# The last store of a rotary embedding, as 120 partitions and two transfers of small pieces

## The chip, the core and the metric

The kernel runs on one core of a Trainium2 chip. The metric is the device time of the program in microseconds, the median of several runs. A profile of one execution lies beside them; its span is the time from the first to the last instruction of the core.

## What is computed

The input `x` is (16, 512, 1024) in fp32: 16 batches, 512 positions, 16 heads of 64. Each head is rotated by its position's angle:

```python
x1, x2 = x[..., :half_dim], x[..., half_dim:]
rotated = concatenate([x1 * cos - x2 * sin, x1 * sin + x2 * cos], axis=-1)
```

with `cos` and `sin` of (512, 32), the same for all batches and heads. 33.55 MB are read and as many written, and little is computed on each.

## The kernel before

The 128 partitions of SBUF each hold some consecutive positions. A *row* `u` is one position of each partition, 128 x 1024 elements, 4 KB a partition; there are 64 rows. They are grouped into ten *tiles*: batches 0, 1, 14 and 15 are tiles of their own (4 rows, 16 KB a partition, 2 MB), and the twelve batches between go in pairs (8 rows, 32 KB a partition, 4 MB). The last tile, number 9, is batch 15, rows 60 to 63.

All tiles live in one ring `x_sb` of 40 rows and are changed in place. ACT issues the loads (`load`, L154): as many as the ring holds at the start, and the others when the store of the rows that they overwrite has ended (L195). Then, for each row:

- VectorE multiplies the row by the cosine into PSUM (`t1_ps`, L302).
- GpSimd multiplies the row, halves swapped, by the signed sine into `t2_sb` (L263), mostly two rows in one instruction; for one row of each pair tile VectorE does it (L295).
- The two are added: for 43 rows VectorE adds them back into `x_sb` (`comb`, L313); for 21 rows TensorE adds `t2` to PSUM through an identity matrix (L225), and ACT copies the sum back (L192).

SP only stores. `on_sync` walks the rows; at the last row of a tile it waits until all rows so far are added (`wait_added`, L138 and its neighbours) and issues one transfer for the tile (L162), ten in all. `in_dram` and `in_sbuf` give the two sides; for the last tile each is 128 rows of 16 KB. The store signals a semaphore, +16 when all of it has landed: one of three that ACT waits for, or `sem_rest` for the last six stores. The last instruction of SP waits for all of `sem_rest` (L163); with that the program ends.

SP's stores and ACT's loads go through queues of their own (q1 and q10 in the profile), which are served by the same 16 DMA engines.

## Time and profile before

| | |
|---|---|
| median of 3 runs | 161.18 us (161.16 to 162.24) |
| the profiled execution | 161.04 us |
| its span | 159.6 us |
| busy: VectorE, GpSimd, TensorE, ACT | 81%, 82%, 40%, 15% of the span |
| DMA: 67.25 MB in 3169 packets | 421 GB/s over the span |
| stores (q1), loads (q10) | 48.9%, 49.8% of the 16 engines' span |
| last store issued | 151.9 us |

The share of a queue is the time that its packets took, over 16 engines and the span; the two together leave 1.3% of the engines' time free. In the tables by window below, the columns are the stretch and its length, the busy time of PE, PEld, DVE, ACT and POOL with the number of instructions, the clock granted to TensorE, the busy share of the DMA engines, and GB/s. A packet is one contiguous run of bytes that a DMA engine moves, or a closing packet of 4 bytes that signals a semaphore.

### The profile page before, as it was taken

How to read it: one execution, taken by the hardware profiler on the slowest of the kernel's cores; microseconds unless marked ns; L12 is line 12 of the kernel's file. 1: busy time of each engine (PE TensorE's matmuls, PEld its weight loads, DVE VectorE, ACT ScalarE, POOL GpSimd, SP SyncE). 2: the span in 40 equal slices, each digit the busy share in tenths (PEclk: the TensorE clock that was granted, in tenths of full speed). 3: DMA queues.
4: the chain of work that ended last, by engine and by line, in shares of the span. 5: the costliest groups of instructions: out<-in, count | busy, mean ns of one | idle time of the engine just before them, and what ended most of it. 6: DMA issues, size and time to landing. Idle time of an engine off the chain costs nothing.

```text
span 159.6 us, 499 instructions
## 1 busy us (share of the span) xinstructions
PE 64.4 (40%) x94; PEld 22.2 (14%) x94; DVE 129.6 (81%) x117; ACT 24.3 (15%) x27; POOL 131.7 (82%) x41
## 2 busy tenths in 40 slices
PE   6050017076408870789067400575058506900000
PEld 1020011021102220222021100211021102300000
DVE  0069947999999989998999629999999999556900
ACT  0420002004300250023102040023202310220000
POOL 1069999999999999999999798992999999089400
PEclk9999999759985589557759985589957995585555
DMA  5999999999999999999999999999999999999997
GB/s 144 396 466 472 394 411 431 448 476 402 394 448 406 495 419 402 476 435 402 443 435 435 394 476 435 402 460 394 427 456 448 443 394 423 472 419 435 386 456 300
DMA packets 3169, 67.25 MB, mean 421 GB/s; under 512 B 352, under 2 KB 608, under 8 KB 608
## 3 DMA queue, kind: packets, MB, share of 16 engines
q10 hardware_dynamic: 1728, 33.69, 49.8%
q1 hardware_dynamic: 1440, 33.56, 48.9%
q14 instruction: 1, 0.01, 0.0%
HBM read 33.69 MB, written 33.55 MB: 421 GB/s over the span
## 4 chain that ended last, share of the span: by engine, by line
DMA 61%; DVE 17%; POOL 5%; PE 5%; issue 4%; ACTq 1%; ACT 1%; DVEq 0%; POOLq 0%; SPq 0%
DMA x_sb<-in_x_dram 43%; DMA out_dram<-x_sb 18%; DVE t_ps L302 8%; DVE x_sb L313 7%; POOL t_sb L263 5%; PE t_ps L225 5%; DVE t_sb L295 2%; ACT x_sb L192 1%; ACTq L154 1%; ACTq L175 1%; DVE tab_ps L280 0%; DVEq L312 0%; DVE tab_ps L281 0%; DVEq L299 0%; POOLq L259 0%
## 5 line engine op out<-in xcount | busy, mean ns | idle before, releaser
L263 POOL TENSOR_TENSOR t_sb<-x_sb,s_sb 128x2048 f32<-128x2048 f32 (+1 forms) x35 | 131.0, 3784 | 17.1 <-DMA x_sb<-in_x_dram 8.3
L225 PE MATMUL t_ps<-t_sb,ident 128*128 128x512 f32 x84 | 59.6, 857 | 69.1 <-DVE t_ps L302 56.7
L302 DVE TENSOR_TENSOR t_ps<-x_sb,pair_ps 128x1024 f32<-128x1024 f32 x48 | 57.5, 1221 | 5.2 <-ACT x_sb L192 5.2
L313 DVE TENSOR_TENSOR x_sb<-t_ps,t_sb 128x1024 f32<-128x1024 f32 x43 | 52.2, 1216 | 5.9 <-POOL t_sb L263 5.9
L192 ACT ACTIVATE x_sb<-t_ps 128x1024 f32<-128x1024 f32 x21 | 21.4, 1024 | 107.6 <-PE t_ps L225 99.9
L225 PEld LDWEIGHTS t_ps<-t_sb,ident 128*128 128x128 f32 x84 | 20.3, 267 | 108.2 <-DVE t_ps L302 78.7
L302 DVE TENSOR_TENSOR t_ps<-x_sb,tab_ps 128x1024 f32<-128x1024 f32 x16 | 19.2, 1222 | 2.6 <-DMA x_sb<-in_x_dram 2.5
L295 DVE TENSOR_TENSOR t_sb<-x_sb,tab_ps 128x1024 f32<-128x1024 f32 x6 | 7.3, 1209 | 0.0
L273 DVE COPY tab_ps<-stage 128x128 f32<-128x128 f32 x1 | 0.3, 296 | 7.6 <-DMA stage<-in_cos_dram 7.6
L209 PE MATMUL pair_ps<-stage,pick 128*128 128x256 f32 x4 | 2.0, 667 | 5.1 <-DMA stage<-in_sin_dram 5.1
L202 PE MATMUL t_ps<-zero 128*128 128x512 bf16 x6 | 2.7, 629 | 1.3 <-DVE zero L271 1.3
L178 ACT ACT_TABLE_LOAD x1 | 1.3, 1283 | 5.5 <-issue 5.5
L209 PEld LDWEIGHTS pair_ps<-stage,pick 128*128 128x128 f32 x4 | 1.2, 324 | 6.1 <-issue 6.0
L202 PEld LDWEIGHTS t_ps<-zero 128*128 128x128 bf16 x6 | 0.7, 136 | 2.4 <-DVE zero L271 1.2
L271 DVE MEMSET zero<- 128x256 uint32 x1 | 0.3, 272 | 0.9 <-PEq L346 0.9
L187 ACT ACTIVATE s_sb<-pair_ps 128x256 f32<-128x256 f32 x1 | 0.4, 384 | 1.7 <-PE pair_ps L209 1.7
L183 ACT ACTIVATE s_sb<-stage 128x128 f32<-128x128 f32 x1 | 0.3, 310 | 1.8 <-DMA stage<-in_sin_dram 1.8
L236 POOL MEMSET ident<- 128x128 f32 x1 | 0.2, 205 | 0.3 <-POOLq L346 0.3
L178 ACT ACTIVATE pick<-ident 128x256 f32<-128x256 f32 x1 | 0.4, 416 | 0.0
L188 ACT ACTIVATE s_sb<-pair_ps 128x256 f32<-128x256 f32 x1 | 0.4, 377 | 0.0
L238 POOL TENSOR_SCALAR_AFFINE_SELECT ident<-ident 128x128 f32<-128x128 f32 x1 | 0.3, 295 | 0.1
L346 POOL MEMSET const-float32-0.0<- 128x1 f32 x1 | 0.1, 99 | 0.3 <-issue 0.3
(6 smaller groups left out, 1.0 us busy)
## 6 DMA issues: line engine op xcount, KB each, us to landing
x_sb<-in_x_dram ACTq DMA_DIRECT2D x6, 4096.0 KB, 38.7
out_dram<-x_sb SPq DMA_DIRECT2D x6, 4096.0 KB, 25.3
x_sb<-in_x_dram ACTq DMA_DIRECT2D x4, 2048.0 KB, 22.7
out_dram<-x_sb SPq DMA_DIRECT2D x4, 2048.0 KB, 16.1
stage<-in_cos_dram ACTq DMA_DIRECT2D x1, 64.0 KB, 7.5
stage<-in_sin_dram ACTq DMA_DIRECT2D x1, 64.0 KB, 7.2
```

Of the source, the lines that this page charges most:

```text
L154: eng.dma_start(in_sbuf(t), in_dram(x1, x2, t)).then_inc(sem_in[t], 16)
L175: ae.dma_start(stage[:, i, :], table.rearrange("(s r) d -> s (r d)", r=R1)).then_inc(sem, 16)
L178: ae.activation(pick[:], ident[:].rearrange("q (s k) -> q k s", k=2)[:, :, :, None].broadcast_to([P, 2, P // 2, 2]), COPY).then_inc(sem_g, 1)
L187: ae.activation(s2[:, :, :, 0, :], pair_ps[:, :, 1, :, :], COPY, scale=-1.0)
L192: ae.activation(xs[:, u % RING, :], t1_ps[:, u % NT1, :], COPY).then_inc(sem_a, 1)
L202: pe.matmul(t1_ps[:, k, b * BANK:(b + 1) * BANK], zero[:, 0:P], zero[:], start=True, stop=True).then_inc(sem_w, 1)
L209: pe.matmul(pair_ps[:, k].rearrange("p c r d -> p (c r d)"), pick[:, k].rearrange("q s b -> q (s b)"), stage[:].rearrange("q c f -> q (c f)"),
L225: ins = pe.matmul(t1_ps[:, u % NT1, b * BANK:(b + 1) * BANK], ident[:], t2[:, b * BANK:(b + 1) * BANK], start=False, stop=True, skip_group ...
L263: pl.tensor_tensor(t2_sb[:, u % NT2:u % NT2 + n], x_sb[:, k:k + n, :, ::-1, :], table[:, :, None, :, :].broadcast_to([P, n, H, 2, HALF]), ...
L295: ve.tensor_tensor(t2_sb[:, u % NT2, :, :, :], swapped(k), over_heads(v_ps), mult)
L302: ve.tensor_tensor(t1_ps[:, u % NT1, :].rearrange("p (h d) -> p h d", d=HALF), x_sb[:, k, :, :, :].rearrange("p h t d -> p (h t) d"), c_of ...
L313: ve.tensor_tensor(xs[:, k, :], t1_ps[:, u % NT1, :], t2_sb[:, u % NT2, :, :, :].rearrange("p h t d -> p (h t d)"), add,).then_inc(sem_v, 1)
```

## The change

The last tile's store no longer goes out as one transfer of 128 rows of 16 KB. `store_last` issues three from SP, one behind the other, without a wait between them. The first has partitions 0 to 119, as before in rows of 16 KB. The partitions 120 to 127 are cut into pieces of 256 elements, 1 KB; of the 16 pieces of each partition the second transfer takes the even ones and the third the odd ones, 8 x 8 = 64 pieces each. All three signal `sem_rest`, and the final wait counts two transfers more. Nothing else is changed.

```diff
+    WHOLE = 120
+    PIECE = 256
...
                 if r == tiles[t][1] - 1:
                     wait_added(sp, u)
                     k = u // R2
+                    if t == NT - 1:
+                        store_last(sp, t)
+                        continue
                     sp.dma_start(in_dram(o1, o2, t), in_sbuf(t)).then_inc(sem_out[k] if k < EARLY else sem_rest, 16)
-            sp.wait_ge(sem_rest, 16 * sum(stores_of(k) for k in range(EARLY, NU // R2)))
+            sp.wait_ge(sem_rest, 16 * (2 + sum(stores_of(k) for k in range(EARLY, NU // R2))))
+
+        def store_last(sp, t):
+
+            dst, src = in_dram(o1, o2, t), in_sbuf(t)
+            sp.dma_start(dst[:WHOLE], src[:WHOLE]).then_inc(sem_rest, 16)
+            for i in range(2):
+                piece = [a[WHOLE:].rearrange("p (q i e) -> p q i e", i=2, e=PIECE)[:, :, i, :] for a in (dst, src)]
+                sp.dma_start(*piece).then_inc(sem_rest, 16)
```

## The prediction

> **What bounds the kernel now.** I read the page first (busy shares and the chain that ended last), then what SP waited for, and then the transfers of the last microseconds. The chain of the page puts the end on transfers:

> ```profile
> DMA 61%; DVE 17%; POOL 5%; PE 5%; issue 4%; ACTq 1%; ACT 1%; DVEq 0%; POOLq 0%; SPq 0%
> ...
> q1 hardware_dynamic: 1440, 33.56, 48.9%
> ```

> The last computation, the sum of row 63 (L313), starts at 150.6 us and takes 1.21; the last store is issued at 151.88. From there nothing but transfers stands before the end:

> ```profile
> SPq L163 <- DMA out_dram<-x_sb: 7.4, 1, 7.4
> ```

> ```profile
> DMA to landing us min/median/max: 7.7/22.7/31.2
> ```

> The first line is SP's wait at the end, the second the store (L162), of which the last has the least, 7.7 us. Its 2,048 KB alone don't fill that time: the window from 151.9 us to the end moved 2.82 MB, so 0.7 MB of older stores went first. The rate is flat to the end:

> ```profile
> 141.20:151.90 10.70, 0.00 (x0) 0.00 (x0) 8.31 (x8) 0.00 (x0) 8.24 (x3) 0.56 0.98 423
> 151.90:158.60 6.70, 0.00 (x0) 0.00 (x0) 0.00 (x0) 0.00 (x0) 0.00 (x0) 0.50 0.98 421
> ```

> The last two columns are the busy share of the 16 DMA engines and GB/s: they are full. The price of a row of 16 KB is in a window (155.2 to 158.2 us) with such packets alone:

> ```profile
> DMA packets 80, 1.31 MB, mean 437 GB/s; under 512 B 0, under 2 KB 0, under 8 KB 0
> ...
> q1 hardware_dynamic: 80, 1.31, 101.8%
> ```

> 1.018 x 16 engines x 3.0 us / 80 = 0.611 us a packet, 27 GB/s an engine. The ten stores made 1440 packets, 144 each: 128 rows and 16 closing ones. So each of 16 lots has eight rows, 8 x 0.611 = 4.89 us. How evenly do the lots end? A packet is booked where it starts:

> ```profile
> 157.70:158.20 0.50, 0.00 (x0) 0.00 (x0) 0.00 (x0) 0.00 (x0) 0.00 (x0) 0.50 1.22 524
> 158.20:158.30 0.10, 0.00 (x0) 0.00 (x0) 0.00 (x0) 0.00 (x0) 0.00 (x0) 0.50 0.00 0
> 158.30:158.60 0.30, 0.00 (x0) 0.00 (x0) 0.00 (x0) 0.00 (x0) 0.00 (x0) 0.50 1.16 492
> 158.60:158.90 0.30, 0.00 (x0) 0.00 (x0) 0.00 (x0) 0.00 (x0) 0.00 (x0) 0.50 0.00 0
> ```

> 524 GB/s x 0.5 us is 16 rows, one per engine; then 492 x 0.3 is nine rows. So seven lots are through at about 158.5 and nine run one row longer, to 158.95 to 159.2. The span ends at 159.6, 0.4 us after the last row. An even end: no lot is much later than the others.

> **The change part by part.** The sum is made against the profiled execution, 161.04 us (span 159.6 and 1.44 around it); the median of the runs shown is 161.18, 0.14 more. What the ten loads, the nine other stores and all engines do before 151.88 us is the same code.

> *The 120 rows.* They replace 128. If they go as 15 lots of eight, a lot costs 4.89 us as now and one engine has none: 0. Below nothing: spread evenly over 16 engines, 7.5 rows, -0.3 us. Above: eight engines with 15 rows each, 7 x 0.611 = +4.3 us. No row shows a transfer that isn't 128 rows; I take 0, since 120 is fifteen of the lots that the trace shows, and keep both ends. [...]

> *The issues.* SP issues three transfers instead of one. An issue lasted 0.34 to 0.62 us (L162), so the last is out by 151.88 + 3 x 0.62 = 153.7. Cover: the older stores and the whole rows hold the engines until 158.5. Cost 0; without that cover 1.2 us. Nothing is queued behind these on SP but the final wait (L163), which now counts 16 x 2 more; two more sets of closing packets follow the data. The rest of the end, 0.4 us from last packet to last instruction, stays.

> *The last eight partitions.* 128 KB go as 2 x 64 pieces of 1 KB, behind the whole rows. The price of a small packet is in the table loads (7.62 to 8.01 us): 512 B each, beside 20 closing packets.

> ```profile
> DMA packets 145, 0.06 MB, mean 164 GB/s; under 512 B 20, under 2 KB 145, under 8 KB 145
> ...
> q10 hardware_dynamic: 145, 0.06, 57.0%
> ```

> 0.57 x 16 x 0.39 us / 125 is at most 28 ns. With 0.611 us for 16 KB that makes 37.6 ns a KB more, so 28 + 19 = 47 ns for 1 KB. On eight engines that is 16 x 47 ns = 0.75 us each, on 16 engines 0.38. But those loads spread over all 128 partitions; the pieces sit in eight. The nearest row for that is a lot of the store: a sixteenth of the partitions moves at 27 GB/s in every store, and no row shows more out of so few. If that is what eight partitions give, the 128 KB take 4.89 us however many engines ask. Between 0.38 and 4.89 I take 2.44, half the upper end: more engines ask than one, yet they ask of one place. [...]

> *The lot that is relieved.* Its engine is free from 154.3 us or earlier. That ends the span sooner only if it was the very last: the last three rows start within the last 0.1 us before 158.6, so -0.1 at most, and 0 if it is another. I take 0.

> *Sum.* The pieces can start at 158.5, when the first lots are through, and the last lots join at 159.2. Shared work of 2.44 us then ends between 160.9 and 161.6, say 161.3, against 159.2 now: +2.1 us. Profiled execution 163.1; on the median of the runs 161.18 + 2.1 = 163.3 us, with its own range of 162.9 to 163.7.

> **The rivals.**

> *The pieces are cheap.* They cost what their packets cost, 0.38 to 0.75 us, on engines of which seven are 0.5 us early. At least one of eight engines is a late one, so the end moves by 0.4 to 0.75: 161.6 to 161.9, centre 161.7 us. For it: every price in the trace is a plain price per packet. Against: all of those were taken with 128 partitions in play.

> *The 120 rows collide.* Sixteen lots run at 0.611 us a row without getting in each other's way. Fifteen lots can cut the partitions at other places, and then two engines draw on what one had for itself. Half speed is 8 x 0.611 = 4.9 us more, and with the pieces at 0.75 to 1.6 (some of them hidden beside lots that end later) +5.6 to +6.5; if half of the slowed time escapes that, 2.45 + 0.75 = +3.2. So 164.4 to 167.7, centre 166.8 us. For it: an even cut in 16 is all that the trace shows; against: nothing in it shows two packets slowing each other. [...]

> *Fewer engines for the 120 rows.* Eight engines, 15 rows: +4.3, with the pieces +5: 166.2 us. Against: 120 divides by 15.

> *Not slower.* The pieces fall to the seven engines that are through at 158.5: they have 0.5 us to spare, so up to ten pieces each at 47 ns vanish, and the relieved engine was the last: -0.1 us, 161.1 us. It decides as long as no late engine gets pieces and none waits. The evidence against is the count: seven engines early, at least eight needed. [...]

> *It does not do what it says.* If the 1 KB pieces were merged into rows again, eight rows of 0.611 would follow on eight engines, +0.6: the time of the cheap rival; the packets would tell.

> **How the numbers follow.** Forecast 0.37 (163.3); collision 0.25 (166.8); cheap or merged pieces 0.18 (161.7); not slower 0.09 (161.1); fewer engines 0.07 (166.2); worse than all of these, with four or more lots on one place, 0.04. The range 161.5 to 167.7 leaves out the not-slower case and the worst one, 0.13, and a little of the edges. A change of this kernel can be told from none at about 1%, 1.6 us. Slower by more: 0.36 of the forecast, 0.25, 0.07 and 0.04, 0.72. Within: 0.01 of the forecast, 0.18, and 0.05 of the not-slower case, 0.24. Faster by more: 0.04, since the whole uneven end is 0.7 us and only something that the trace doesn't show could give 1.6.

> **What would show it.** The stores' packets should be 9 x 144 + 120 + 15 + 2 x 72 = 1575 (merged pieces: fewer). Up to about 158.5 us the windows should be those of before with 15 rows a beat instead of 16; if the rate falls to half right after 153.6, the 120 rows collide or sit on fewer engines. After the last whole row, 0.13 MB should take about 2.4 us, near 55 GB/s; at 0.4 to 0.75 us the cheap rival is right. SP's final wait should grow from 7.4 us to about 8.5 (2.1 longer, and begun one microsecond later), and the three issues should stand close together from 151.9. The forecast is wrong if the end moves by less than 1.5 us or more than 2.8.

## The result and the profile after

The change made the kernel slower: 165.46 us (median of 6 runs, 165.26 to 165.65) against 161.17 before, a ratio of 1.0254 with a 95% interval of 1.0228 to 1.028. That is +4.3 us; the profiled execution took 165.65 us with a span of 164.2.

The packet counts of the page show that the transfers were made as written, and over how many engines:

```profile
DMA packets 3304, 67.25 MB, mean 410 GB/s; under 512 B 367, under 2 KB 751, under 8 KB 751
...
q1 hardware_dynamic: 1575, 33.56, 49.3%
```

1575 packets on the stores' queue are 9 x 144 and 120 + 15 and 2 x (64 + 8). The packets under 512 B are the closing ones, 16 for each of the other 21 transfers: 367 = 21 x 16 + 15 + 8 + 8. Read as one for each engine of a transfer, the 120 rows went in 15 lots and each set of pieces over eight engines, as the forecast had it. A store of eight rows in the last but one experiment fits this reading: it closed with eight packets, and its rows of 0.62 us all lay in one window of 0.7 us with them, so they ran at once.

Where the time went is seen in windows of the changed kernel (columns as before, the last two the engines' busy share and GB/s):

```profile
141.20:151.90 10.70, 0.08 (x1) 0.00 (x0) 8.40 (x8) 1.02 (x1) 8.45 (x3) 0.75 0.97 420
151.90:153.70 1.80, 0.00 (x0) 0.00 (x0) 0.12 (x1) 0.00 (x0) 0.00 (x0) 0.50 1.04 437
153.70:158.60 4.90, 0.00 (x0) 0.00 (x0) 0.00 (x0) 0.00 (x0) 0.00 (x0) 0.50 1.00 284
158.60:160.10 1.50, 0.00 (x0) 0.00 (x0) 0.00 (x0) 0.00 (x0) 0.00 (x0) 0.50 0.78 218
160.10:163.90 3.80, 0.00 (x0) 0.00 (x0) 0.00 (x0) 0.00 (x0) 0.00 (x0) 0.50 0.52 134
```

Until 153.7 us the rate is that of the kernel before. Then, when the 120 rows begin, the engines are as busy as before (1.00) and move a third less, 284 GB/s where the kernel before moved 421 to the end. A busy engine at a lower rate means longer packets. In the window of 155.2 to 158.2 us, which held 80 rows before, there are now 48 and one closing packet:

```profile
DMA packets 49, 0.79 MB, mean 262 GB/s; under 512 B 1, under 2 KB 1, under 8 KB 1
...
q1 hardware_dynamic: 49, 0.79, 98.7%
```

0.987 x 16 x 3.0 us / 48 = 0.99 us a row, where it was 0.611. That points to the rival in which the 120 rows collide. The issues took longer than thought, and that stayed hidden:

```profile
152.10 0.40 SPq L173 DMA_DIRECT2D out_dram<-x_sb  x1
152.55 3.59 SPq L176 DMA_DIRECT2D out_dram<-x_sb  x2
```

The two sets of pieces needed 0.83 and 2.72 us to issue (the least and the most of L176). The last was out at 156.1, still before 158.9, when the first lot of rows closed.

### The profile page after: what moved, and what is told of

Same layout as the page of the kernel before. It is cut to its first block, busy times and chain, and to the rows that moved or that the text cites. A ratio compares the mean times of both kernels' runs of the same rounds, so it can differ in the third digit from the quotient of the medians.

```text
span 164.2 us, 501 instructions
## 1 busy us (share of the span) xinstructions
PE 68.0 (41%) x94; PEld 23.3 (14%) x94; DVE 129.7 (79%) x117; ACT 24.2 (15%) x27; POOL 131.6 (80%) x41
## 3 DMA queue, kind: packets, MB, share of 16 engines
q1 hardware_dynamic: 1575, 33.56, 49.3%
## 4 chain that ended last, share of the span: by engine, by line
DMA 59%; DVE 15%; PE 6%; POOL 5%; issue 4%; ACTq 1%; ACT 1%; DVEq 0%; POOLq 0%; SPq 0%
DMA x_sb<-in_x_dram 41%; DMA out_dram<-x_sb 17%; DVE t_ps L315 7%; DVE x_sb L326 7%; PE t_ps L238 6%; POOL t_sb L276 5%; DVE t_sb L308 1%; ACT x_sb L205 1%; ACTq L156 1%; ACTq L188 1%; DVE tab_ps L293 0%; DVEq L325 0%; DVE tab_ps L294 0%; POOLq L272 0%; DVEq L312 0%
## 5 line engine op out<-in xcount | busy, mean ns | idle before, releaser
L238 PE MATMUL t_ps<-t_sb,ident 128*128 128x512 f32 x84 | 63.2, 906 | 66.9 <-DVE t_ps L315 54.6
L238 PEld LDWEIGHTS t_ps<-t_sb,ident 128*128 128x128 f32 x84 | 21.4, 282 | 108.6 <-DVE t_ps L315 77.7
```

Of the source, the lines that this page charges most:

```text
L238: ins = pe.matmul(t1_ps[:, u % NT1, b * BANK:(b + 1) * BANK], ident[:], t2[:, b * BANK:(b + 1) * BANK], start=False, stop=True, skip_group ...
```

## The experiments

Theory A: the 120 rows are cut so that lots get in each other's way. Theory B is the forecast: the rows cost nothing, and the eight partitions do. Times are medians, each with the kernel before on the same chip: 161.46 us for the first four runs, 161.25 and 161.26 for the later timed ones. The diffs show the lines that matter; the count of the final wait follows what is issued.

**The 120 rows alone.**

```diff
             sp.dma_start(dst[:WHOLE], src[:WHOLE]).then_inc(sem_rest, 16)
-            for i in range(2):
-                piece = ...
-                sp.dma_start(*piece).then_inc(sem_rest, 16)
```

> The last tile's store is the 120-partition transfer alone; the partitions 120 to 127 of the last tile are left unwritten. Theory A (the 120 rows are cut into lots that get in each other's way): the loss stays, +3.4 to +4.3 us on before, 164.6 to 165.5 us. Theory B (the forecast: the rows are free, the pieces of eight partitions cost about 2.4 us, and whatever else the change lost lies with the pieces or their issue): nothing is left, 161.0 to 161.4 us.

Measured: 164.96 us, ratio 1.0221 (1.0185 to 1.0258), +3.5 us, although 6% of the last tile is never stored. Theory A holds and theory B falls: most of the loss is in the 120 rows. The pieces add 0.5 us to it in the change by the medians, 0.8 us by the two losses; the intervals overlap. The rate falls here as in the change, with no pieces at all:

```profile
153.70:158.60 4.90, 0.00 (x0) 0.00 (x0) 0.00 (x0) 0.00 (x0) 0.00 (x0) 0.50 0.92 264
```

**Eight whole rows in place of the pieces.**

```diff
-            for i in range(2):
-                piece = ...
-                sp.dma_start(*piece).then_inc(sem_rest, 16)
+            sp.dma_start(dst[WHOLE:], src[WHOLE:]).then_inc(sem_rest, 16)
```

> The 120 rows as in the change, and the eight partitions behind them in one plain transfer of eight rows of 16 KB. Theory A: about the time of the change, 165.0 to 166.0 us, since the pieces were not what cost. Theory B: 128 KB out of eight partitions at the pace of two lots, 163.0 to 163.7 us if the cut into 1 KB is harmless, and 161.8 us if the small pieces alone were dear.

Measured: 166.08 us, ratio 1.0287 (1.0268 to 1.0307). It is as slow as the change, if not slower, so neither the small pieces nor the third issue is to blame.

**The pieces alone**, behind an even store of 128 rows:

```diff
+            sp.wait_ge(sem_out[0], 16 * stores_of(0))
+            sp.dma_start(dst, src).then_inc(sem_rest, 16)
             for i in range(2):
-                piece = [a[WHOLE:].rearrange(...)[:, :, i, :] for a in (dst, src)]
+                piece = [a[WHOLE:].rearrange(...)[:, :, i, :] for a in (o1[0], src)]
                 sp.dma_start(*piece).then_inc(sem_rest, 16)
```

> The last store is one transfer of 128 rows as before; behind it go the two transfers of 64 pieces as extra work, written over the same partitions' part of batch 0 (128 KB that then hold batch 15's numbers). This is the pieces alone, behind an even store. If the eight partitions are one place that all eight engines share (the forecast's term): +2.0 to +2.4 us, 163.2 to 163.6 us. If the pieces cost what a packet costs: +0.4 to +0.8, 161.6 to 162.0 us. Theory A allows both, theory B only the first or more.

Measured: 163.26 us, ratio 1.0119 (1.0098 to 1.0141), +1.8 us, just under the +2.0 to +2.4 named. The forecast's term for the pieces was near the truth, if nothing hides them. A window with pieces and closing packets alone (159.4 to 160.8 us of this run):

```profile
DMA packets 83, 0.08 MB, mean 54 GB/s; under 512 B 9, under 2 KB 83, under 8 KB 83
...
q1 hardware_dynamic: 83, 0.08, 43.1%
```

0.431 x 16 x 1.4 us / 74 = 0.13 us for 1 KB, nearly three times the 47 ns that the prediction worked out, and 54 GB/s in all: the worth of two engines at the 27 GB/s of a row, though eight work by the closing packets.

**The same pieces from partitions that are not neighbours.**

```diff
-                piece = [a[WHOLE:].rearrange(
+                piece = [a[0:32:4].rearrange(
```

> As the run with the extra pieces, with the same 2 x 64 pieces of 1 KB on eight partitions, taken from the partitions 0, 4, 8, ..., 28 in place of 120 to 127 (written over the same partitions' part of batch 0, which then holds batch 15's numbers). Sharing of a place by neighbouring partitions: with each partition in another group of four the pieces cost their packets alone, +0.4 to +0.9 us on before, 161.6 to 162.2 us. If what cost was eight partitions as such, the eight engines, the writing side or the small pieces: the same as with neighbours, 163.0 to 163.5 us.

Measured: 161.88 us, ratio 1.0033 (1.0005 to 1.0062), +0.6 us, near the 0.75 us that 16 packets at 47 ns come to. The window of 159.4 to 159.8 us:

```profile
DMA packets 41, 0.04 MB, mean 95 GB/s; under 512 B 4, under 2 KB 41, under 8 KB 41
...
q1 hardware_dynamic: 41, 0.04, 27.2%
```

0.272 x 16 x 0.4 us / 37 = 47 ns. The pieces are the same in number and size and go over as many engines: of the 16 + 8 + 8 closing packets at the end, the windows hold 30 here (158.5 to 160.0 us) and 31 in the run before (158.6 to 161.3). What differs is the partitions, and with them the rows of batch 0 that are written. So the small pieces took 0.13 us each from neighbouring partitions and 47 ns from these; that the cause is in SBUF and not in the rows written, this run alone doesn't show.

**Two transfers of 64 partitions.**

```diff
+            for h in (slice(0, 64), slice(64, 128)):
+                sp.dma_start(dst[h], src[h]).then_inc(sem_rest, 16)
```

> The last store as two transfers of 64 partitions each, partitions 0 to 63 and then 64 to 127, rows of 16 KB as before, all data written. Both counts divide by 16. Theory A in its wide form (paths belong to groups of partitions, and a transfer that doesn't span all 128 has engines sharing them): each half goes at half rate, +4 to +5 us, 165.2 to 166.2 us. Theory A in its narrow form (only the cut into 15 is bad): 161.0 to 161.8 us, as under theory B.

Measured: 165.28 us, ratio 1.0238 (1.0209 to 1.0267), +3.8 us. All rows are in play here, and by the closing packets all 16 engines: the window from 153.7 to 163.7 us has 45, nine more than in the run with the eight whole rows, as 2 x 16 is nine more than 15 + 8. So the odd number 15 isn't the cause; 64 neighbouring partitions lose as well. The engines are busy, and the rate is that of the run with the 120 rows alone:

```profile
153.70:158.60 4.90, 0.00 (x0) 0.00 (x0) 0.00 (x0) 0.00 (x0) 0.00 (x0) 0.50 1.05 264
```

**Two transfers of 128 partitions**, a control:

```diff
+            for h in (slice(0, 2048), slice(2048, 4096)):
+                sp.dma_start(dst[:, h], src[:, h]).then_inc(sem_rest, 16)
```

> The last store as two transfers of all 128 partitions, the first and the second half of each row of 16 KB (8 KB rows). A control: it has a second issue and second closing packets, and no lots that collide. Theory A: 160.9 to 161.5 us, equal or a little earlier, since half as long packets let the lots end closer together. If a second transfer at the end itself costs (its issue, its closing): 161.7 to 162.5 us.

Measured: 161.38 us, ratio 1.0005 (0.9991 to 1.0018). A second issue and a second closing cost nothing here; the hoped-for more even end brought nothing either.

**SBUF or DRAM?** The kernel before with one more copy at its end, within SBUF, of 128 and of 120 partitions:

```diff
+            src, dst = in_sbuf(NT - 1), in_sbuf(NT - 2)
+            sp.dma_start(dst[:128], src[:128]).then_inc(sem_copy, 16)   # 120 in the other
+            sp.wait_ge(sem_copy, 16)
```

> The kernel before, and after its end one more transfer within SBUF, the 128 partitions of the last tile copied to the place of the tile before it (2 MB, no DRAM on either side). Reference for the next run: 16 lots of eight rows, 4.9 us and a start and landing of about 2 us, so 167 to 169 us.

> The same copy within SBUF with 120 partitions. If the lots of 15 collide on the SBUF side: 3 to 5 us longer than with 128 partitions, 170.5 to 173.5 us. If the collision is on the DRAM side (how 15 engines walk the output): no longer than with 128, 167 to 169 us.

Measured: 169.6 and 174.33 us, one execution each. SP's wait for the copy, first with 128 and then with 120 partitions:

```profile
SPq L167 <- DMA x_sb<-x_sb: 7.9, 1, 7.9
```

```profile
SPq L167 <- DMA x_sb<-x_sb: 12.0, 1, 12.0
```

+4.1 us of waiting for 6% less data (+4.7 us in the whole time, as the second issue took about 1.0 us and the first 0.5: 13.0 and 8.4 us from issue to landing, less the waits), with no DRAM on either side. So the 120 rows collide on the SBUF side. Both times lie above the ranges expected: a row lasted 0.84 us on the mean in the first copy and 1.22 in the second, so even the copy of 128 partitions was slower than 0.611 us a row. Why was not taken apart. Start and landing took about 1.7 us in the first copy (8.4 from issue to landing, less 8 x 0.84), where about 2 had been expected.

**Partitions 16 apart.**

```diff
-                piece = [a[0:32:4].rearrange(
+                piece = [a[0:128:16].rearrange(
```

> As the run with the spread pieces, now from the partitions 0, 16, 32, ..., 112 (again written over the same partitions' part of batch 0). No two are neighbours. If a place is a group of four neighbours and nothing else, the pieces cost 42 to 47 ns a packet as at 0, 4, ..., 28: +0.5 to +0.7 us, 161.7 to 162.0 us. If partitions 32 apart share a place too (which would make lots of eight neighbours collide in pairs), two partitions share each of four places and the packets take about 80 ns: +1.0 to +1.4 us, 162.2 to 162.7 us.

Measured: 162.59 us (162.09 to 163.31), ratio 1.0083 (1.0057 to 1.0108), +1.3 us. The time fits the second reading, but it doesn't settle the question: pieces ran beside the last whole rows. From 159.4 to 159.9 us of the profiled execution 34 pieces and three rows took 5.4 us of engine time together; with the pieces at 80 ns the rows lasted 0.9 us, with the rows at 0.611 us the pieces 0.10, so what shared with what can't be told. The next run was made for that.

**One by one.** Five stores after the end, each alone:

```diff
+            for n, h in enumerate((slice(120, 128), slice(0, 32, 4), slice(0, 128, 16), slice(0, 120), slice(0, 128))):
+                sp.dma_start(dst[h], src[h]).then_inc(sem_copy, 16)
+                sp.wait_ge(sem_copy, 16 * (n + 1))
```

> The kernel before, and after its end five more stores from the last tile over batch 0 (which then holds batch 15's numbers), each waited for before the next, so that nothing else is in flight; rows of 16 KB throughout: (1) partitions 120 to 127; (2) 0, 4, ..., 28; (3) 0, 16, ..., 112; (4) 0 to 119; (5) 0 to 127. What counts is how long a row lasts. If a place is four neighbours and the same four 32 higher: (1) four rows share, about 2.4 us a row; (2) none, 0.61; (3) two share, about 1.22; (4) most rows at about 1.2, the transfer 8 to 10 us of rows; (5) 0.61, 4.9 us of rows. If a place is four neighbours alone: the same but (3) at 0.61, and then (4) can't come from lots of eight neighbours. If neither, and 8 or 15 engines are slow as such: (1), (2) and (3) alike.

Measured: 187.49 us, one execution. The five stores in windows of their own:

```profile
160.40:163.10 2.70, 0.00 (x0) 0.00 (x0) 0.00 (x0) 0.00 (x0) 0.00 (x0) 0.50 0.44 49
164.80:165.50 0.70, 0.00 (x0) 0.00 (x0) 0.00 (x0) 0.00 (x0) 0.00 (x0) 0.50 0.44 187
167.10:168.40 1.30, 0.00 (x0) 0.00 (x0) 0.00 (x0) 0.00 (x0) 0.00 (x0) 0.50 0.45 101
169.50:179.30 9.80, 0.00 (x0) 0.00 (x0) 0.00 (x0) 0.00 (x0) 0.00 (x0) 0.50 0.85 201
180.50:185.60 5.10, 0.00 (x0) 0.00 (x0) 0.00 (x0) 0.00 (x0) 0.00 (x0) 0.50 0.97 411
```

The rates of the windows, their ends included, agree with the reading: 49 GB/s is 24.5 for each of two places, 101 is 25 for each of four, and 187 is 23 for each of eight.

**The change one tile earlier.**

```diff
-                    if t == NT - 1:
+                    if t == NT - 2:
                         store_last(sp, t)
```

> The change moved one tile earlier: tile 8 (batch 14) goes out as 120 rows and 2 x 64 pieces, tile 9 whole as before. Loads are just over and the rest of tile 7's store is in flight when it is issued, 11 us before the last store. If the time that colliding rows cost is lost to the engines, the last store queues behind it on every engine: +2.5 to +4.5 us, 163.8 to 165.8 us. If 11 us are enough to hide it: 161.1 to 161.8 us.

Measured: 167.73 us, ratio 1.0383 (1.0344 to 1.0422), +6.5 us: it isn't hidden in the time before the last store, 9.2 us in this run, and costs more than at the end and 2 us more than the upper bound. In the kernel before the DMA engines are 98% busy there and move 423 GB/s; from 149 to 152 us of this run they moved 213 to 262, so what was queued behind the slow rows came later. The end is also more uneven. Two windows of the last microseconds:

```profile
164.00:165.00 1.00, 0.00 (x0) 0.00 (x0) 0.00 (x0) 0.00 (x0) 0.00 (x0) 0.50 0.15 66
165.00:166.00 1.00, 0.00 (x0) 0.00 (x0) 0.00 (x0) 0.00 (x0) 0.00 (x0) 0.50 0.15 66
```

That is 0.15 x 16, two or three engines, still at rows of 0.611 us while the others are through. How much of the extra 2 us this is wasn't taken apart.

## Why the prediction was right or wrong

The direction and the range held (161.5 to 167.7). The forecast time, 163.3, was 2.2 us short: half of the loss was seen, and for the wrong reason. That the range held is luck as far as the forecast's own mechanism goes: it had been drawn to take in the rival that came true.

- *The 120 rows*: the step that failed. The value taken was 0, "since 120 is fifteen of the lots that the trace shows". The lots' number and size were right (15 closing packets, eight rows each); that they run side by side at 0.611 us was not. Alone, the 120 rows fill a window of 9.8 us where 128 fill one of 5.1; at the end of the kernel they cost +3.5. The prediction had the parts at hand, fifteen lots of eight and, in a rival, two engines that draw on what one had for itself, and held to 0 because no row showed it. The bound above, +4.3, had been worked out for eight engines, which was not the cause, and happens to hold.
- *The last eight partitions*: 2.44 us was the term, the author's estimate at half of one lot's 4.89 us; no transfer of the trace of before shows it. The runs showed 2.4 us for the same 128 KB as eight rows by themselves, and for the pieces behind even lots +1.8, with 54 GB/s in all near the 55 named in the forecast. But in the change it didn't come on top: the lots of the 120 rows end spread out (the first closes at 158.9 us, data moves until 163.9), so few engines were at their pieces at one time: in the change's trace 1.9 pieces ran at once on the mean, six at most, and the 128 pieces took 53 ns on the mean. The change is only 0.5 to 0.8 us over the 120 rows alone.
- *The issues*: 0 was right, the durations were not: up to 2.72 us where 0.62 was the longest row to go by. The last issue still ended 2.8 us before the first lot closed. SP's final wait was 8.0 us, near the 8.5 foreseen, but by luck: it began about 3 us later than thought and ended 2.5 us later.
- *The lot that is relieved*: it could not show, as the end was set by other lots.
- *The rivals*: "The 120 rows collide" was the mechanism, at a chance of 0.25 and 166.8 us, 1.3 us too much: it counted half speed for all rows, while in the change's trace 50 of the last 120 to start took no more than 0.70 us. Its sign in the trace was named beforehand, a rate that falls right after 153.6 us; it fell from 437 to 284 GB/s, not to half. "The pieces are cheap" and "Fewer engines for the 120 rows" fell with the runs on the pieces and the count of closing packets, and the 1575 packets show that the pieces were not merged into rows.

What misled was reading that 16 lots run "without getting in each other's way" as a property of the engines. By these runs it belongs to the cut: with 128 partitions all 16 engines run rows of 0.61 us at once, as if each had a place in SBUF for itself.

## What to carry to other kernels

A store's engines can all be busy and still move less: 284 GB/s at a share of 1.00 in the change where 437 stood before, and alone 201 at 0.85 for 120 partitions against 411 at 0.97 for 128. Compare the time of one packet (0.99 us against 0.611), not the busy share. By these runs, keep a large DMA between SBUF and DRAM on all 128 partitions, and if it has to be split, split along the row (two halves of each row cost nothing here), not along the partitions (64 + 64 cost 3.8 us, 120 + 8 cost 4.3). Few partitions that must go alone should not be neighbours: 128 pieces from eight neighbours cost 1.8 us, from 0, 4, ..., 28 only 0.6. Being apart is not enough, though: from 0, 16, ..., 112 they cost 1.3.

## What the runs showed of the hardware that was not expected

Issuing a transfer of 64 small pieces kept SP for 0.83 to 2.72 us, against 0.34 to 0.66 us for a transfer of 128 rows in the same kernel. The pieces alone don't explain it: the transfer of eight whole rows behind the 120 took about 2.1 us to issue, while the five stores issued one by one, with nothing in flight, took an estimated 0.5 us each (20.4 us from the first issue to the end of the fifth, less the waits between them: 25.1 in all, of which the first, before any of the five, is put at the 7.4 of the kernel before). The cause is open. A piece of 1 KB taken with others from eight neighbouring partitions lasted 0.13 us on the mean, where from 0, 4, ..., 28 it lasted 47 ns. And a collision's price isn't paid once: one tile earlier the same three transfers cost 6.5 us instead of 4.3.
